# Centring all four pairs by float32r pairs, behind the attention projection's first tile

## The chip, the cores and the metric

One core of one Trainium2 chip runs the whole kernel. The metric is device time in microseconds (us), the median of several runs. The engines that matter are TensorE (PE, the matmuls; PEld is its weight load, which overlaps them), VectorE (DVE), ScalarE (ACT), GpSimd (POOL) and SyncE (SP), which here issues the loads of weights.

## What is computed

One layer of a streaming encoder with 512 tokens of 1024 features: a half-step SwiGLU, two token mixers side by side whose outputs are gated and merged, another half-step SwiGLU, and a last RMS norm. The change lies where the two mixers end. Mixer A is a delta-rule recurrence (RWKV-7) with 8 heads of 64; its output `y` is normalised per head, scaled, given a bonus, and multiplied by a gate. Mixer B is forgetting attention, also 8 heads of 64.

```python
# end of mixer A: y is (tokens, 8 heads, 64)
mu = mean(y, axis=-1); var = mean(square(y - mu), axis=-1)     # per head
y = (y - mu) * rsqrt(var + LNX_EPS)
y = y * lnx_g + lnx_b
y = (y + bonus) * (sigmoid(g_lo) @ g_up)
y_a = y @ rwkv_proj                    # 512 -> 1024
y_b = attention_output @ fox_proj      # 512 -> 1024
x = x + (sigmoid(g_A) * y_a + sigmoid(g_B) * y_b) @ w_out
```

## The kernel before, in words

Features lie on the 128 partitions and the 512 tokens along the free dimension, so a tile is 128x512 in f32, one PSUM bank. A matmul of f32 accuracy is made of float32r parts: a value is split into a high half (a cast on ACT) and a low half (a subtraction on DVE), and `mm3` (L174 to L177) adds high by high, high by low and low by high. A single matrix that is exact in float32r needs only the two parts of the other operand: `exact` (L191), two matmuls. A plain f32 matmul shows in the trace as two passes.

The stretch at issue runs from `gslot` (L1991) to `written(False)` (L2091). Two heads make a pair, so mixer A's output is four tiles `vs[0]` to `vs[3]`, slices of one buffer `V4`. For each pair p:

- `first(p)` multiplies `vs[p]` by the matrix `center` (identity less 1/64 within a head), into the bank `ycs[p]`, which comes from a PSUM pool of three (`pr`). Before, pairs 0 to 2 do this as one plain f32 matmul, and pair 3 by `exact` with a split `parts["y"]`.
- `squared(p)` squares the bank on ACT, `parts_of` or `halved` splits the square.
- `second(p)`, the norm round, sums the squares over a head (`pg`, two matmuls) and opens the gate by three float32r matmuls of the split gate codes `gl` (also named `pg` in the trace).
- `logs(p)` takes Ln and Exp on ACT, which gives 1/sqrt; `divided(p)`, `shaped(p)` and `opened(p)` are three DVE steps over `vs[p]`, and `halves_of(p)` splits the result into `ya[p]` for the RWKV projection.

Beside this runs the attention projection: `proj(m, fox_proj, ...)` for eight output tiles m, 12 matmuls each into the bank `ppj`. Its weights come by `weights()`: a load on SP into one of three raw buffers, the high half `whi` on ACT, the low half `wlo` on DVE, both with two buffers. `gated(m)` multiplies a tile by its gate on DVE and frees the bank. The loop over m lays `second`, `logs` and the steps of `ROUNDS[m]` between the tiles.

Within this stretch `dve`, `act` and `pe` are `Queued`: each instruction is put behind the one before it on its engine, so that each of the three runs in the order of the text. All of them carry line L103 in the trace, where `Queued` calls the engine; they are told apart by their tiles. The planner's list ahead of it (`plan.run(ORDER, PLACES)`, L1975) ends with the last merge gate, whose product with `rstd` (`gs`) is the last DVE instruction of that list. Instructions outside, such as the RWKV projection's weights (L167 and L168), the residual loads of POOL (L2113) and the gates' tanh (`late_tanh`, L2105), are placed by a scheduler; the first three tanh only behind `parted`, the last ACT instruction at the point m = 4 of the loop.

After the stretch comes the RWKV projection, `proj(m, rwkv_proj, ya)` for eight tiles, then the output projection and the second SwiGLU.

Of the kernel before, what the change touches and what calls it, by code (L numbers as in the profile page):

```python
# [10 lines left out]
F32R = mybir.dt.float32r  # L11
# [8 lines left out]
P = 128  # L20
T = 512
# [5 lines left out]
NP = DA // P  # L27
# [15 lines left out]
COL_Q = COL_W + 160  # L43
# [39 lines left out]
def kernel(  # L83
# [24 lines left out]
    dve, act, pe = [Queued(e, False) for e in (nc.vector, nc.scalar, nc.tensor)]  # L108
# [14 lines left out]
    def bank(name, pool_=None):  # L123
        pool_ = pool_ or pm
        return pool_.tile([P, T], F32, tag="b", name=name)

    def tmp(name, shape=(P, T), dt=F32, tag="t", **kw):
        return tp.tile(list(shape), dt, tag=tag, name=name, **kw)
# [14 lines left out]
    center = cp.tile([P, P], F32R, name="center")  # L143
# [13 lines left out]
    def load_raw(aps, kt, n):  # L157
        raw = wp.tile([P, kt, n], F32, tag="raw", name="raw", bufs=3)
        for c0, src in aps:
            loads.append(nc.sync.dma_start(raw[:, :, c0:c0 + src.shape[1]],  # L160
                                           src.rearrange("(k p) c -> p k c", p=P)))
        return raw

    def split_w(raw, kt, n, eng=None, hi_eng=None):
        hi = wp.tile([P, kt, n], F32R, tag="whi", name="whi", bufs=2)
        lo = wp.tile([P, kt, n], F32R, tag="wlo", name="wlo", bufs=2)
        (hi_eng or act).copy(hi[:], raw[:])  # L167
        (eng or dve).tensor_tensor(lo[:], raw[:], hi[:].bitcast(F32), op=ALU.subtract)  # L168
        return hi, lo
# [4 lines left out]
    def mm3(ps, whi, wlo, xhi, xlo, first, last, onto=False):  # L174
        pe.matmul(ps, whi, xhi, start=first, stop=False, skip_group_check=onto)  # L175
        pe.matmul(ps, whi, xlo, start=False, stop=False, skip_group_check=onto)  # L176
        return pe.matmul(ps, wlo, xhi, start=False, stop=last, skip_group_check=onto)  # L177
# [7 lines left out]
    def parts_of(src):  # L185
        hi, lo = tmp("shi", dt=F32R), tmp("slo", dt=F32R)
        act.copy(hi[:], src)
        dve.tensor_tensor(lo[:], src, hi[:].bitcast(F32), op=ALU.subtract)
        return hi, lo

    def exact(ps, mat, src, parts=None):  # L191
        hi, lo = parts or parts_of(src)
        pe.matmul(ps, mat[:], hi[:], start=True, stop=False)
        pe.matmul(ps, mat[:], lo[:], start=False, stop=True)

    def split(dst_hi, dst_lo, src, hi_eng="act"):
        cast = act.copy(dst_hi, src) if hi_eng == "act" else dve.tensor_copy(dst_hi, src)
        return cast, dve.tensor_tensor(dst_lo, src, dst_hi.bitcast(F32), op=ALU.subtract)

    def f32(ap):  # L200
        return ap.bitcast(F32)
# [115 lines left out]
    with tc.tile_pool(name="x0", bufs=1) as x0:  # L317
# [99 lines left out]
        for c in range(2, KD):  # L417
# [14 lines left out]
            elif c == 6:  # L432
                second = [split_w(load_raw([(0, ffn1_w1[0][:, P:2 * P])], KD, P), KD, P, qdve, hi_eng=qact)]
# [70 lines left out]
    class Seven:  # L504
# [12 lines left out]
        def second(s, g):  # L517
            d = s.lo[g][:, :, TH:]
            dve.tensor_tensor(d, d, s.hi[g][:, :, TH:], op=ALU.subtract)
# [131 lines left out]
    class Wide:  # L651
# [226 lines left out]
        def gated(s, j):  # L878
            h, t = s.seven.hidden(j), s.sa[j]
            act.activation(t, t, AF.Silu)  # L880
            dve.tensor_tensor(h, h, t, op=ALU.mult)
# [231 lines left out]
    with ExitStack() as mx:  # L1113
# [68 lines left out]
        lg = tmp("lg")  # L1182
# [33 lines left out]
        for o, c0, mu in ((spare[2], DA, 4), (spare[3], 0, 0)):  # L1216
            ps = bank("pk", pf)
# [3 lines left out]
        for p in range(NP):  # L1221
            za.append((zslots[2 * p], zslots[2 * p + 1]))
            for i, (w_, x_, par0, o) in enumerate(((uw, lw, PAR_W0, zslots[2 * p]), (ux, lx, PAR_A0, zslots[2 * p + 1]))):
                ps = bank("pz", (pr, pf)[i])
# [3 lines left out]
        logs = tc.keep_in_program_order(act.preload_act_table_set("natural_log_exp_and_others"))  # L1228
# [4 lines left out]
        t2 = pctx.enter_context(tc.tile_pool(name="t2", bufs=1, side="right"))  # L1233
# [8 lines left out]
        vs = [V4[:, p] for p in range(NP)]  # L1242
# [154 lines left out]
        t2 = fctx.enter_context(tc.tile_pool(name="fx", bufs=1, side="right"))  # L1397
# [8 lines left out]
        for t in range(C - 1):  # L1406
            n, m = t + 1, C - 1 - t
# [20 lines left out]
        class Rows(Columns):  # L1428
# [8 lines left out]
            def weights(s):  # L1437
                super().__init__("pq", s.at)
# [518 lines left out]
        ybs = []  # L1957
# [19 lines left out]
        def proj_w(m, wt):  # L1977
            return load_w([(0, wt[0][:, m * P:(m + 1) * P])], NP, P)

        def proj(m, wt, y, w=None):  # L1980
            wh, wl = w or proj_w(m, wt)
            ps = bank("ppj")
            for k in range(NP):
                mm3(ps[:], wh[:, k, :], wl[:, k, :], y[k][0], y[k][1], k == 0, k == NP - 1)
            return ps
# [9 lines left out]
        gup, lg, bons = gslot[10], gslot[11], gslot[12:16]  # L1995
# [5 lines left out]
            nc.gpsimd.dma_start(gslot[m], gsave[KD + m])  # L2001
        fws = [proj_w(0, fox_proj)]
        ycs, sqs, pgs, pus, parts = [None] * NP, [None] * NP, [None] * NP, [None] * NP, {}
        gl = [t2.tile([P, T], F32R, name=f"gl{i}", tag=tag) for i, tag in enumerate(("kb1", "klc0", "klc1", "qb1"))]

        def first(p):
            ycs[p] = bank("yc", pr)
            if p < NP - 1:
                pe.matmul(ycs[p][:], f32(center[:]), vs[p], start=True, stop=True)
            else:  # L2010
                exact(ycs[p][:], center, None, parts["y"])

        def squared(p):
            sqs[p] = gslot[8 + p % 2]
            act.activation(sqs[p], ycs[p][:], AF.Square)
# [9 lines left out]
        def logs(p):  # L2025
            rn = tslot[p]
            act.activation(rn, pgs[p][:], AF.Ln, bias=epsl[:, 0:1], scale=1.0 / 64)
            act.activation(rn, rn, AF.Exp, scale=-0.5)
# [14 lines left out]
            squared(p)  # L2043
            parts[p] = parts_of(sqs[p])

        ROUNDS = ((divided, 0), (shaped, 0), (opened, 0)), ((fourth, 3), (halves_of, 0), (divided, 1), (shaped, 1)),                  ((opened, 1), (divided, 2), (shaped, 2)), ((opened, 2), (halves_of, 1)),                  ((halves_of, 2), (divided, 3)), ((shaped, 3), (opened, 3)), ((halves_of, 3),), ()

        def gated(m, ps):
            g = gslot[m] if m + 1 < KD else gs
# [8 lines left out]
        def halved(src, tags):  # L2058
            hi, lo = [t2.tile([P, T], F32R, name="shi", tag=tag) for tag in tags]
            split(hi[:], lo[:], src)  # L2060
            return hi, lo

        parts["y"] = halved(vs[3], [f"qk{COL_Q}{i}" for i in range(2)])
        weights()
        for p in range(3):
            first(p)
        for p in range(2):
            squared(p)
            parts[p] = parts_of(sqs[p])
        for i, src in enumerate((gup, lg)):  # L2070
            split(gl[2 * i][0:96, :], gl[2 * i + 1][0:96, :], src[0:96, :])
        squared(2)
        parts[2] = halved(sqs[2], [f"qk{COL_Q}{i}" for i in range(2, 4)])
        ps = proj(0, fox_proj, ybs, fws[0])
        for m in range(KD):
            if m < NP:
                second(m)
            gated(m, ps)
            if m + 2 < KD:
                weights()  # L2080
            if m < NP:
                logs(m)
            if m == NP:
                parted = act.last
            for do, p in ROUNDS[m]:
                do(p)
            if m + 1 < KD:
                ps = proj(m + 1, fox_proj, ybs, fws[m + 1])
            if m == 0:
                first(3)  # L2090
        written(False)  # L2091
        fctx.close()
# [25 lines left out]
        for m in range(KD):  # L2118
            g = slot[m]
            ps = proj(m, rwkv_proj, ya)  # L2120
# [4 lines left out]
        for m in range(KD):  # L2125
            wh, wl = load_w([(0, w_out[0][:, m * P:(m + 1) * P])], KD, P)
            ps = bank("pw")
# [69 lines left out]
    with tc.tile_pool(name="hp", bufs=1) as hp:  # L2197
# [5 lines left out]
        ps = [bank("pa"), bank("pb", pr)]  # L2203
# [51 lines left out]
```

## Time and profile before

| | us |
|---|---|
| median of 3 runs | 1066.22 |
| lowest and highest | 1064.59, 1066.35 |
| the profiled execution | 1066.64 |
| its span in the trace | 1064.9 |
| PE busy in the span | 1054.1 |
| DVE, ACT, POOL busy | 842.8, 712.0, 243.4 |

The profile is of one execution. Its span lies 1.7 us below that execution's own time, which includes what lies around the span, and the execution lies 0.42 us above the median. Starts are given from the span's start. A matmul's listed duration includes its way through the array: matmuls that follow each other without a gap start 0.227 us apart but last 0.39, so a bank is complete 0.39 us after its last matmul's start. The chain's times are those of ends, some tenths later than the timeline's starts.

### The profile page before, as it was taken

The numbers are of one execution on the slowest core, as the hardware profiler recorded it, in microseconds if no ns is written. First come the engines' busy times: TensorE is split into PE (matmuls) and PEld (weight loads), VectorE is DVE, ScalarE is ACT, GpSimd is POOL, SyncE is SP. The second block draws the span as 40 slices with busy tenths as digits, with TensorE's granted clock in tenths as the row PEclk, the third lists the DMA queues.
The fourth block names the chain that finished last, engine by engine and source line by source line (L and its number), as shares of the span: only waits on it lengthen the run. The fifth ranks groups of instructions, "written<-read, shape, count | busy, mean of one in ns | idle before, by whom it ended". The sixth has DMA issues, their size and how long they took to land.

```text
span 1064.9 us, 16739 instructions
## 1 busy us (share of the span) xinstructions
PE 1054.1 (99%) x6178; PEld 863.2 (81%) x6178; DVE 842.8 (79%) x1171; ACT 712.0 (67%) x1107; POOL 243.4 (23%) x291
## 2 busy tenths in 40 slices
PE   9999999999999999999999999999999999999997
PEld 7888888888887887878777877888888888888886
DVE  7997776789865698878989878866797766799874
ACT  6767868776555766435888766554578868676554
POOL 1221220134203201312012231136321212115210
PEclk9999999999999999999999999999999999999999
DMA  7989989889945433443335565566989999979972
GB/s 213 264 181 237 231 201 255 198 194 193 232 123 170 116 112 97 129 121 117 86 74 125 130 177 164 189 167 163 283 200 204 208 239 232 201 212 206 236 186 79
DMA packets 194960, 190.25 MB, mean 179 GB/s; under 512 B 64958, under 2 KB 131070, under 8 KB 194878
## 3 DMA queue, kind: packets, MB, share of 16 engines
q1 hardware_dynamic: 147230, 110.78, 36.3%
q0 software_dynamic: 33392, 70.14, 34.2%
q10 hardware_dynamic: 14256, 8.26, 2.7%
q8 instruction: 49, 0.80, 0.3%
q14 instruction: 33, 0.27, 0.1%
HBM read 163.51 MB, written 12.52 MB: 165 GB/s over the span
## 4 chain that ended last, share of the span: by engine, by line
PE 92%; DVE 4%; DMA 1%; ACT 1%; issue 1%; SPq 0%; DVEq 0%; ACTq 0%; POOL 0%; POOLq 0%
PE P L103 39%; PE P L177 6%; PE P L176 6%; PE P L175 6%; PE pgt L103 5%; PE spot L103 3%; PE pq L103 3%; PE l L103 2%; PE ppj L103 2%; PE pb L103 2%; PE pa L103 2%; PE pk L175 1%; PE pk L176 1%; PE pw L176 1%; PE pk L177 1%; PE pw L177 1%
## 5 line engine op out<-in xcount | busy, mean ns | idle before, releaser
L103 PE MATMUL P<-sraw,q 128*128 128x512 f32 x344 | 91.3, 389 | 0.0
L103 PEld LDWEIGHTS P<-sraw,q 128*128 128x128 f32 x344 | 64.6, 188 | 13.4
L103 PE MATMUL P<-swhi,q 128*128 128x512 f32 x224 | 71.2, 389 | 0.0
L167 ACT CAST whi<-raw 128x1024 fp32r<-128x1024 f32 (+2 forms) x42 | 40.3, 960 | 44.1 <-issue 14.2
L103 PE MATMUL P<-sraw,wxh 128*128 128x512 f32 x200 | 67.7, 390 | 0.0
L694 POOL DMA_DIRECT2D cb<-in_ffn_w_dram x20 | 24.1, 1207 | 142.3 <-DVE cd L103 74.9
L103 PE MATMUL P<-swhi,wxh 128*128 128x512 f32 x144 | 56.6, 393 | 0.0
L168 DVE TENSOR_TENSOR wlo<-raw,whi 128x1024 fp32r<-128x1024 f32 (+2 forms) x43 | 48.4, 1126 | 10.1 <-ACT whi L167 8.9
L103 PE MATMUL P<-swhi,wxl 128*128 128x512 f32 x144 | 56.1, 390 | 0.0
L103 PE MATMUL P<-swlo,wxh 128*128 128x512 f32 x144 | 56.1, 389 | 0.0
L694 POOL DMA_DIRECT2D cd<-in_ffn_w_dram x24 | 29.3, 1221 | 115.3 <-DVE swlo L103 37.9
L103 PE MATMUL P<-sraw,wxl 128*128 128x512 f32 x136 | 52.9, 389 | 0.0
L103 PEld LDWEIGHTS P<-swhi,q 128*128 128x128 f32 x224 | 42.0, 188 | 8.8 <-DVE q L103 0.2
L103 ACT COPY RD<-spot 32x128 f32<-32x128 f32 (+2 forms) x128 | 39.8, 311 | 11.3 <-PE spot L103 9.3
L103 DVE TENSOR_TENSOR u<-P,u 128x512 f32<-128x512 f32 x52 | 33.4, 682 | 17.2 <-ACT u L103 17.2
L103 PEld LDWEIGHTS P<-sraw,wxh 128*128 128x128 f32 x200 | 37.5, 188 | 7.8
L103 PE MATMUL P<-swlo,q 128*128 128x512 f32 x112 | 43.6, 389 | 0.0
L552 POOL DMA_DIRECT2D ca<-in_ffn_w_dram x16 | 19.3, 1205 | 96.1 <-DVE swlo L103 66.7
L177 PE MATMUL pk<-xh,wlo 128*128 128x512 f32 x96 | 37.5, 392 | 1.0 <-DVE wlo L168 1.0
L175 PE MATMUL pk<-xh,whi 128*128 128x512 f32 x96 | 38.1, 397 | 0.4 <-DVE u L1261 0.4
L176 PE MATMUL pk<-xl,whi 128*128 128x512 f32 x96 | 37.5, 390 | 0.0
L177 PE MATMUL P<-swhi,wxl 128*128 128x512 f32 x96 | 37.3, 389 | 0.0
(632 smaller groups left out, 3445.6 us busy)
## 6 DMA issues: line engine op xcount, KB each, us to landing
cc<-in_ffn_w_dram SPq DMA_DIRECT2D x36, 512.0 KB
cb<-in_ffn_w_dram POOLq DMA_DIRECT2D x36, 512.0 KB, 6.6
cb<-in_ffn_w_dram SPq DMA_DIRECT2D x32, 512.0 KB
cd<-in_ffn_w_dram POOLq DMA_DIRECT2D x32, 512.0 KB, 7.5
ca<-in_ffn_w_dram POOLq DMA_DIRECT2D x32, 512.0 KB, 8.7
raw<-in_w_in_dram SPq DMA_DIRECT2D x27, 512.0 KB
ca<-in_ffn_w_dram SPq DMA_DIRECT2D x20, 512.0 KB
cd<-in_ffn_w_dram SPq DMA_DIRECT2D x18, 512.0 KB
```

Of the source, the lines that this page charges most:

```text
L103: q.last = do(*a, **kw)
L167: (hi_eng or act).copy(hi[:], raw[:])
L168: (eng or dve).tensor_tensor(lo[:], raw[:], hi[:].bitcast(F32), op=ALU.subtract)
L175: pe.matmul(ps, whi, xhi, start=first, stop=False, skip_group_check=onto)
L176: pe.matmul(ps, whi, xlo, start=False, stop=False, skip_group_check=onto)
L177: return pe.matmul(ps, wlo, xhi, start=False, stop=last, skip_group_check=onto)
L552: nc.gpsimd.dma_start(s.sum[g], src, accum_op=ALU.add)
L694: nc.gpsimd.dma_start(to, s.block(b, n, h), accum_op=ALU.add)
```

## The change

All four pairs are centred by `exact`, with the split of their outputs made ahead by `centred(p, tags)`. The first attention tile goes ahead of the centrings of pairs 0 to 2. The squares and splits that follow, and the split gate codes, move to m = 0 behind `gated(0)`; pair 3's output is split at m = 0 too and centred behind tile 2 instead of tile 1. `second` and `logs` are called one tile later, for m from 1 to 4 instead of 0 to 3, and `ROUNDS` is moved by one tile, with the last steps drawn together: `shaped(3)` joins `divided(3)` at m = 5, and `opened(3)` and `halves_of(3)` stand together at m = 6. The tiles `gl` are taken only after the centrings, since two of their buffers hold the split of pair 2 before.

```diff
-        gl = [t2.tile([P, T], F32R, name=f"gl{i}", tag=tag) for i, tag in enumerate(("kb1", "klc0", "klc1", "qb1"))]
+        gl = []
         def first(p):
             ycs[p] = bank("yc", pr)
-            if p < NP - 1:
-                pe.matmul(ycs[p][:], f32(center[:]), vs[p], start=True, stop=True)
-            else:
-                exact(ycs[p][:], center, None, parts["y"])
+            exact(ycs[p][:], center, None, parts["y", p])
...
-        ROUNDS = ((divided, 0), (shaped, 0), (opened, 0)), ((fourth, 3), (halves_of, 0), (divided, 1), (shaped, 1)),                  ((opened, 1), (divided, 2), (shaped, 2)), ((opened, 2), (halves_of, 1)),                  ((halves_of, 2), (divided, 3)), ((shaped, 3), (opened, 3)), ((halves_of, 3),), ()
+        ROUNDS = (), ((divided, 0), (shaped, 0), (opened, 0)), ((fourth, 3), (halves_of, 0), (divided, 1), (shaped, 1)), \
+            ((opened, 1), (divided, 2), (shaped, 2)), ((opened, 2), (halves_of, 1)), \
+            ((halves_of, 2), (divided, 3), (shaped, 3)), ((opened, 3), (halves_of, 3)), ()
...
-        parts["y"] = halved(vs[3], [f"qk{COL_Q}{i}" for i in range(2)])
+        def centred(p, tags):
+            parts["y", p] = halved(vs[p], tags)
+
+        quarters = [f"qk{COL_Q}{i}" for i in range(4)]
+        for p, tags in enumerate((quarters[0:2], quarters[2:4], ("kb1", "klc0"))):
+            centred(p, tags)
         weights()
+        ps = proj(0, fox_proj, ybs, fws[0])
         for p in range(3):
             first(p)
-        for p in range(2):
-            squared(p)
-            parts[p] = parts_of(sqs[p])
-        for i, src in enumerate((gup, lg)):
-            split(gl[2 * i][0:96, :], gl[2 * i + 1][0:96, :], src[0:96, :])
-        squared(2)
-        parts[2] = halved(sqs[2], [f"qk{COL_Q}{i}" for i in range(2, 4)])
-        ps = proj(0, fox_proj, ybs, fws[0])
         for m in range(KD):
-            if m < NP:
-                second(m)
+            if 0 < m <= NP:
+                second(m - 1)
             gated(m, ps)
+            if m == 0:
+                for p in range(2):
+                    squared(p)
+                    parts[p] = parts_of(sqs[p])
+                gl.extend(t2.tile([P, T], F32R, name=f"gl{i}", tag=tag) for i, tag in enumerate(("kb1", "klc0", "klc1", "qb1")))
+                for i, src in enumerate((gup, lg)):
+                    split(gl[2 * i][0:96, :], gl[2 * i + 1][0:96, :], src[0:96, :])
             if m + 2 < KD:
                 weights()
-            if m < NP:
-                logs(m)
+            if m == 0:
+                squared(2)
+                parts[2] = halved(sqs[2], quarters[2:4])
+                centred(3, quarters[0:2])
+            if 0 < m <= NP:
+                logs(m - 1)
             if m == NP:
                 parted = act.last
             for do, p in ROUNDS[m]:
                 do(p)
             if m + 1 < KD:
                 ps = proj(m + 1, fox_proj, ybs, fws[m + 1])
-            if m == 0:
+            if m == 1:
                 first(3)
```

## Rows read from the trace of the kernel before

**Rows 1.** The page, part 1: busy time, share of the span, instructions of each engine.
```profile
PE 1054.1 (99%) x6178; PEld 863.2 (81%) x6178; DVE 842.8 (79%) x1171; ACT 712.0 (67%) x1107; POOL 243.4 (23%) x291
```
**Rows 2.** The chain that ended last, 620 to 700 us: start, us, what.
```profile
643.11 2.58 PE yc L103 x6
645.69 2.77 PE ppj L103 x12
...
649.61 2.75 PE ppj L103 x12
...
660.60 1.15 PE pg L103 x5
661.75 10.91 PE ppj L103 x48
```
**Rows 3.** Timeline of PE, 636 to 676 us: start, us, engine, line, out<-in.
```profile
642.95 2.74 PE L103 MATMUL yc<-V,center 128*128 128x512 f32 x6
...
648.30 0.39 PE L103 MATMUL pg<-shi,bonesr 128*128 128x512 f32 x1
...
652.19 0.62 PE L103 MATMUL yc<-shi,center 128*128 128x512 f32 x2
...
664.33 0.39 PE L103 MATMUL ppj<-yh,whi 128*128 128x512 f32 x1
...
672.49 0.39 PE L175 MATMUL ppj<-ya,whi 128*128 128x512 f32 x1
```
**Rows 4.** Timeline of DVE, the same stretch; in brackets idle before and releaser.
```profile
643.15 0.69 DVE L103 TENSOR_TENSOR gs<-pgt,rstd 128x512 f32<-128x512 f32 x1 [1.50 <-PE pgt L103]
643.76 0.68 DVE L103 TENSOR_TENSOR wlo<-raw,whi 128x512 fp32r<-128x512 f32 x1
...
647.05 1.28 DVE L103 TENSOR_TENSOR gl<-G,gl 96x512 fp32r<-96x512 f32 x2
...
650.44 0.68 DVE L103 TENSOR_TENSOR V<-yc,Tall 128x512 f32<-128x512 f32 x1
```
**Rows 5.** Timeline of ACT, the same stretch.
```profile
640.22 0.62 ACT L103 CAST whi<-raw 128x512 fp32r<-128x512 f32 x1
...
642.92 0.62 ACT L103 CAST whi<-raw 128x512 fp32r<-128x512 f32 x1 [1.56 <-PE pgt L103]
644.01 0.60 ACT L103 ACTIVATE G<-yc 128x512 f32<-128x512 f32 x1 [0.47 <-PE yc L103]
...
649.02 0.68 ACT L103 ACTIVATE Tall<-pg,epsl 128x512 f32<-128x512 f32 x1
649.73 0.63 ACT L103 ACTIVATE Tall<-Tall 128x512 f32<-128x512 f32 x1
```
**Rows 6.** Timeline of DVE at an earlier PE wait, 417 to 426 us.
```profile
423.89 1.22 DVE L168 TENSOR_TENSOR wlo<-raw,whi 128x1024 fp32r<-128x1024 f32 x1
```
**Rows 7.** Timeline of PE at the same wait.
```profile
425.16 0.50 PE L177 MATMUL pk<-xh,wlo 128*128 128x512 f32 x1 [0.68 <-DVE wlo L168]
425.50 0.40 PE L175 MATMUL pk<-xh,whi 128*128 128x512 f32 x1
```
**Rows 8.** DMA issues, 630 to 680 us: count, KB each, median us to landing.
```profile
G<-gsave POOLq DMA_DIRECT2D x5, 256.0 KB, 5.4
```
**Rows 9.** Timeline of ACT toward the end of the stretch.
```profile
664.30 0.62 ACT L103 CAST whi<-raw 128x512 fp32r<-128x512 f32 x1 [1.34 <-PE ppj L103]
664.83 0.61 ACT L103 CAST ya<-V 128x512 fp32r<-128x512 f32 x1
665.46 1.28 ACT L2105 ACT_TABLE_LOAD   x1
666.76 1.68 ACT L2105 ACTIVATE ga<-ga 128x512 f32<-128x512 f32 x3
668.34 0.60 ACT L103 CAST whi<-raw 128x512 fp32r<-128x512 f32 x1
```
**Rows 10.** Timeline of DVE toward the end of the stretch.
```profile
671.57 0.68 DVE L168 TENSOR_TENSOR wlo<-raw,whi 128x512 fp32r<-128x512 f32 x1
672.17 0.68 DVE L103 TENSOR_TENSOR ya<-V,ya 128x512 fp32r<-128x512 f32 x1
```

## The prediction

> **What bounds the kernel now.** I read the page first, then the chain of work that ended last, then the timelines of TensorE (PE), VectorE (DVE) and ScalarE (ACT) around the edit. PE is busy for 99% of the span [rows 1], so a microsecond of PE streaming that goes, or a PE wait that comes, moves the end by about as much. The chain shows the same at the edit: PE alone from the centring matmuls to the first RWKV projection tile, with no other engine between [rows 2]. In this stretch everything on DVE, ACT and PE is chained in the order in which the code writes it. DVE shows that the chain is strict: it idles 1.50 us until the last gate column is out of PE (`gs`), and only then splits the first projection weight (`wlo`), whose high half ACT had written three microseconds before [rows 4, 5].
>
> **The passes.** Before, three plain f32 centrings run as six passes of 2.58 us together [rows 2]. The float32r pairs need six passes too, at the pace of the other float32r matmuls, 10.91/48 = 0.227 us, so 1.36 us. The gain is 1.22 us, on PE, so on the path. Pair 3 has its float32r pair already and keeps it. Nothing else on PE changes in size.
>
> **The first tile ahead of the centrings.** It would start at 642.95, where the centrings start now [rows 3]. Its first two matmuls read the high weight, ready since 640.8 [rows 5]. The third reads the low weight, and is due at 643.40. DVE finishes that at 643.76 + 0.68 = 644.44, behind `gs` [rows 4]; `gs` waits for the gate's last matmul, which the edit doesn't touch. Today the 2.58 us of centrings cover this wait; that cover is gone. What a PE wait for such a weight costs is shown elsewhere in the trace: a low weight written at 423.89 + 1.22 = 425.11, its matmul at 425.16, the next at 425.50, 0.39 us after the write [rows 6, 7]. So the fourth matmul starts at 644.83 instead of 643.63: **+1.20 us**. The ends: nothing, if DVE splits the weight in its idle 1.50 us (a rival below), and 1.5 us, that idle row, if the pick-up is worse. I take 1.20. Gain and wait cancel: the tile and the centrings end at 648.30 - 1.22 + 1.20 = 648.28, where the tile alone ends now [rows 3]. The three casts and low halves of the pairs' outputs that come ahead cost nothing: ACT idles 1.56 us up to 642.92 in the trace [rows 5], and DVE writes the low halves at 644.4 to 646.3 behind `wlo`, before PE needs the first at 646.9.
>
> **The squares, one step later.** Pair 0's square needs its centring, whose second pass starts at 646.9 + 0.23 and ends 0.39 later, so it starts at 647.6 instead of 644.01 [rows 5]. ACT's list behind it is the old one with two casts more (the fourth weight, pair 3's output), 0.53 us each in a run of casts [rows 9]. DVE's low halves of the gate codes (`gl`) move as much: 647.05 + 3.57 = 650.62, both done at 651.9 [rows 4]. PE reaches the first norm round (`pg`) after tile 1 of 2.75 us [rows 2], at 651.03, and its fourth matmul, due at 651.71, reads the last of these halves. It waits to 651.95: **+0.24 us** (0 to 0.5, by what ACT's list may slip).
>
> **Pair 3's centring and its bank.** `first(3)` takes the PSUM bank of pair 0 out of a pool of three, so it waits for `divided(0)`. Now this is done a microsecond before it is needed (650.44 + 0.68 against 652.19 [rows 3, 4]). After the change ACT's Ln for pair 0 comes at 649.02 + 3.57 + 1.06 = 653.65, its Exp 0.71 later, done at 655.0, and `divided(0)` at 655.07 to 655.75 [rows 4, 5]. PE, with 1.15 us for a norm round [rows 2], is through tile 2 at 651.03 + 1.15 + 0.24 + 2.75 = 655.17 and waits to 655.80: **+0.63 us** (0.3 to 1.0). Everything behind it on PE, norm round 1 and tile 3, is delayed by this.
>
> Up to here the sum is -1.22 + 1.20 + 0.24 + 0.63 = **+0.85 us**. The weights' loads on SyncE keep their order; each is released by the low half three tiles earlier, 7.5 us or more ahead of its cast, and a transfer of 256 KB lands in 5.4 us [rows 8], so none becomes late. GpSimd's residual loads wait for pair 3's low half and move with it; the whole RWKV projection, 22 us, lies ahead of their first use.
>
> **The tail.** Round 3 now stands one tile nearer to the RWKV projection. In the trace the table load and three tanh go between a cast and the last attention weight (`whi` at 668.34) [rows 9], and they may start only behind ACT's last instruction at m = 4, which the edit makes Exp of pair 3. Tile 5 starts at 664.33 + 0.85 = 665.18 [rows 3], round 3 1.15 ahead of it, at 664.03; its Ln comes 0.23 + 0.39 us later and a hand-over behind, at 664.7, Exp at 665.4, pair 1's cast at 666.0, table and tanh at 666.6 to 669.6 (1.28 + 1.68 us), the weight's cast at 669.5, its low half at 670.1 to 670.8. PE needs that at 671.1, so it just holds. But behind it DVE's order now has pair 2's low half, `divided(3)`, `shaped(3)`, the gate of tile 6 and `opened(3)`, at 0.60 us a start and 0.71 where one reads the last (before, only three of the five came behind it). The first RWKV weight's low half (L168, not in the chain) stands right ahead of pair 3's low half in the trace [rows 10], so it would follow `opened(3)`: 673.9 to 674.6. PE begins the RWKV projection at 672.49 + 0.85 = 673.34 [rows 3] and needs it at 673.79; its fourth matmul starts at 674.58 + 0.39 = 674.97 instead of 674.02. **+0.95 us**, between 0 (the weight's cast ahead of a tanh) and 2.35 (a rival).
>
> In the trace the first tanh starts 0.02 us after the table load's end, and the load 0.02 after the cast before it [rows 9]. The Trainium skill, "ScalarE: Activation LUTs", What ACT_TABLE_LOAD costs, gives each switch a drain of about 1380 ns beside the load's 1283 ns. By that the tail's wait would be 0.95 + 1.38 = 2.33 us and the change +3.2 us, as an estimate from that page; the load's length agrees with the row, the drain has no place in it.
>
> **The sum.** -1.22 + 1.20 + 0.24 + 0.63 + 0.95 = +1.8 us. The profiled execution took 1066.64 us with a span of 1064.9; it would take 1068.4. It lies 0.42 us above the median of the runs, 1066.22, so I forecast **1068.0**.
>
> **Rivals.**
> *No wait in the tail* (1067.1, chance 0.27): the last attention weight's cast goes ahead of one or two tanh, whose place the scheduler chooses; each is worth 0.53 us. For it: the cast's buffer is free from 668.1 (tile 5's end), before the second tanh. Against it: in the trace all three went ahead, though the buffer was free at 667.2.
> *A longer tail* (1069.4, chance 0.13, slower than before): the first RWKV weight's low half is put behind pair 3's low half. That needs `opened(3)`, a cast of 0.62 and itself, so it ends at 675.4, the weight's at 676.0, and PE loses 2.35 us instead of 0.95: +3.2 us. It decides from the moment at which DVE finds pair 3's cast done when `opened(3)` ends. Against it: in the trace the weight goes ahead [rows 10].
> *The first tile doesn't wait* (1065.9 to 1066.8, chance 0.10): DVE splits the first weight ahead of `gs`. Then all comes 1.2 us earlier: -1.22 + 0.24 + 0.63 = -0.35, with the tail's 0.95 or without. Against it: the chain's order, unedited, kept DVE idle 1.50 us.
> *ACT stands still behind the table load* (1069.3, chance 0.02): if it does so for as long as the load itself, 1.28 us [rows 9], the last attention weight and all behind it on DVE come that much later, PE loses 0.95 + 1.28 = 2.23 us there, and the change costs 3.1 us. The two rows 0.02 us apart speak against it. This is the drain of the Trainium skill's page named above.
> *The pure gain* (1065.0, chance 0.04): the passes go and no wait appears; this needs both the order of DVE and ACT's list to be otherwise.
>
> **How the numbers follow.** The forecast has 0.44. Below it lie 1067.1, 1066.4 and 1065.0, above it 1069.4. A difference of about 0.2%, 2.1 us, is what a measurement of this kernel can tell from no change. No case gains that much; 0.02 is left for what I don't see. Slower by that: the longer tail (0.13), the still table (0.02) and the part of the forecast in which the bounds of the waits and the runs' own spread (1064.59 to 1066.35) add half a microsecond, a fifth of 0.44: 0.24. The rest, 0.74, is no difference. From 1065.7 to 1069.5 are nearly all of the forecast and of the case without the tail's wait, over half of the two outer ones: 0.8.
>
> **What would show it.** Centring passes at 0.23 us in one row of six behind the first tile; a PE wait of over a microsecond on `wlo` at the first tile's third matmul; short PE waits at the first norm round and at pair 3's centring, the latter named after DVE `V`; and a PE wait on L168's `wlo` in the first RWKV tile. If the first of these waits is missing, the forecast is wrong by 1.2 us; if the last is, by 0.95.

## The result, and the profile after

| us | before | after |
|---|---|---|
| median (lowest to highest), 13 runs each | 1065.83 (1064.59 to 1069.11) | 1067.59 (1066.25 to 1068.66) |
| ratio, 95% interval | | 1.0017, 1.001 to 1.0024 |
| the profiled execution, its span | 1066.64, 1064.9 | 1067.78, 1066.1 |
| the stretch of the edit | 51.30 | 53.08 |

The change costs 1.76 us by the medians. The forecast was 1.8 us, at 1068.0 from a median of 1066.22; the 13 runs put that median at 1065.83.

A single profiled execution differs from the next by a microsecond or two, so the spans alone are too coarse here. I therefore measure one stretch in each trace. It begins where the first matmul after the last gate column is due (0.227 us behind the start of that column's last matmul, tile `pgt`) and ends with the start of the output projection's first matmul (tile `pw`). All that the edit moves lies in it. It grew by 53.08 - 51.30 = 1.78 us, which agrees with the medians. Behind it both executions take the same time to the end of the span, 370.7 and 370.6 us. The spans differ by 1.2 us only because this execution of the changed kernel reached the stretch 0.57 us earlier.

The page of the changed kernel, part 1, beside [rows 1]:

```profile
PE 1053.5 (99%) x6178; PEld 862.2 (81%) x6178; DVE 845.1 (79%) x1174; ACT 713.9 (67%) x1110; POOL 244.7 (23%) x291
```

PE is busy for 0.6 us less, in a span 1.2 us longer: streaming went, waiting came. DVE and ACT have three instructions more each, the low and high halves of three pairs' outputs.

The chain that ended last, changed kernel, 636 to 680 us (start, us, what), beside [rows 2]:

```profile
643.19 0.69 DVE wlo L103
643.93 2.60 PE ppj L103 x10
...
647.03 0.61 ACT G L103
...
653.38 0.68 DVE G L103
654.06 0.60 DVE wlo L103
654.66 0.61 DVE V L103
655.32 0.73 PE yc L103 x2
```

Before, this stretch was PE from end to end. Now the chain leaves PE twice. It passes over DVE's split of the first weight, and then over ACT and DVE from the first centring's square to the step `divided(0)` (`V`), which frees the bank of pair 3's centring.

The timeline of PE, changed kernel (start, us, engine, line, out<-in, count; in brackets the idle time and its releaser), beside [rows 3]:

```profile
642.61 0.39 PE L103 MATMUL ppj<-yl,whi 128*128 128x512 f32 x1
643.93 0.50 PE L103 MATMUL ppj<-yh,wlo 128*128 128x512 f32 x1 [0.93 <-DVE wlo L103]
644.27 0.40 PE L103 MATMUL ppj<-yh,whi 128*128 128x512 f32 x1
...
646.37 1.57 PE L103 MATMUL yc<-shi,center 128*128 128x512 f32 x6
647.77 0.40 PE L103 MATMUL ppj<-yh,whi 128*128 128x512 f32 x1
...
650.96 1.18 PE L103 MATMUL pg<-gl,gl 96*128 96x512 f32 x3
651.98 0.40 PE L103 MATMUL ppj<-yh,whi 128*128 128x512 f32 x1
...
654.49 0.39 PE L103 MATMUL ppj<-yh,wlo 128*128 128x512 f32 x1
655.32 0.73 PE L103 MATMUL yc<-shi,center 128*128 128x512 f32 x2 [0.44 <-DVE V L103]
655.89 0.40 PE L103 MATMUL pg<-shi,bonesr 128*128 128x512 f32 x1
...
672.81 0.39 PE L103 MATMUL ppj<-yh,wlo 128*128 128x512 f32 x1
673.18 0.47 PE L175 MATMUL ppj<-ya,whi 128*128 128x512 f32 x1
...
676.61 0.39 PE L176 MATMUL ppj<-ya,whi 128*128 128x512 f32 x1
```

Read it by the distance between starts, since a matmul's listed length hides short waits. Without a wait it is 0.227 us. What goes beyond that, with the 0.1 us by which the next matmul still lags after a wait:

- the six passes: 647.77 - 646.37 = 1.40 us instead of 2.58, so **-1.18**
- the first tile's third matmul: 643.93 - 642.61 - 0.23 = 1.09, and 0.11 at the next, **+1.20**
- norm round 0: 651.98 - 650.96 = 1.02 for three matmuls of 0.68, **+0.34**
- pair 3's centring: 0.60 and 0.12 behind it, **+0.72**
- the beginning of the RWKV projection: 676.61 - 672.81 = 3.80 for fourteen matmuls of 0.227, **+0.6** in four small waits with what lags behind them

The sum is +1.7. The trace's list of PE waits names only the first and the third of them, 0.93 and 0.44 us, because it counts from the modelled end of the matmul before. The others show in the distances, and in the timeline of the weight loads (PEld), which gives the idle time before each load and its releaser:

```profile
651.41 0.30 PEld L103 LDWEIGHTS pg<-gl,gl 96*128 96x128 f32 x2 [0.48 <-DVE gl L103]
...
673.15 0.19 PEld L175 LDWEIGHTS ppj<-ya,whi 128*128 128x128 f32 x1 [0.38 <-issue]
...
673.69 0.19 PEld L177 LDWEIGHTS ppj<-ya,wlo 128*128 128x128 f32 x1 [0.24 <-DVE wlo L168]
...
675.67 0.19 PEld L176 LDWEIGHTS ppj<-ya,whi 128*128 128x128 f32 x1 [0.30 <-DVE ya L103]
...
676.27 0.19 PEld L175 LDWEIGHTS ppj<-ya,whi 128*128 128x128 f32 x1 [0.30 <-DVE G L103]
```

The idle time of a load isn't PE's loss: the load at 673.69 stood for 0.24 us, and its matmul started in time, only the next one 0.08 late. "issue" stands where the profile shows no releaser.

The timeline of DVE in the changed kernel, beside [rows 4, 10]:

```profile
643.19 0.68 DVE L103 TENSOR_TENSOR wlo<-raw,whi 128x512 fp32r<-128x512 f32 x1
...
650.07 1.28 DVE L103 TENSOR_TENSOR gl<-G,gl 96x512 fp32r<-96x512 f32 x2
...
654.58 0.68 DVE L103 TENSOR_TENSOR V<-yc,Tall 128x512 f32<-128x512 f32 x1
...
672.35 0.68 DVE L103 SCALAR_TENSOR_TENSOR G<-G,ppj 128x512 f32<-128x512 f32 x1
672.95 0.68 DVE L168 TENSOR_TENSOR wlo<-raw,whi 128x512 fp32r<-128x512 f32 x1
673.55 0.68 DVE L103 TENSOR_TENSOR V<-V,pg 128x512 f32<-128x512 f32 x1
```

And that of ACT toward the end of the stretch, beside [rows 9]:

```profile
665.62 0.60 ACT L103 CAST ya<-V 128x512 fp32r<-128x512 f32 x1
666.24 1.28 ACT L2113 ACT_TABLE_LOAD   x1
667.54 1.67 ACT L2113 ACTIVATE ga<-ga 128x512 f32<-128x512 f32 x3
669.12 0.60 ACT L103 CAST whi<-raw 128x512 fp32r<-128x512 f32 x1
```

Each of the first three PE waits ends a twentieth of a microsecond behind a DVE write. The weight's low half is done at 643.19 + 0.68 = 643.87, PE goes on at 643.93; `divided(0)` is done at 655.26, PE goes on at 655.32. The gate codes are done at 650.07 + 1.28 = 651.35; PE's row groups the three matmuls, but the weight load of the one that waited starts at 651.41. In the tail the order on ACT is as in [rows 9] (cast, table load, three tanh, then the last attention weight's cast), only now DVE's list behind that weight ends so late that PE meets it.

### The profile page after: what moved, and what is told of

It reads as the page before. It is cut to its first block, busy times and chain, and to the rows that moved or that the text cites. A ratio compares the mean times of both kernels' runs of the same rounds, so it can differ in the third digit from the quotient of the medians.

```text
span 1066.1 us, 16746 instructions
## 1 busy us (share of the span) xinstructions
PE 1053.5 (99%) x6178; PEld 862.2 (81%) x6178; DVE 845.1 (79%) x1174; ACT 713.9 (67%) x1110; POOL 244.7 (23%) x291
## 4 chain that ended last, share of the span: by engine, by line
PE 92%; DVE 4%; ACT 1%; DMA 1%; issue 1%; SPq 0%; DVEq 0%; ACTq 0%; POOL 0%; POOLq 0%
PE P L103 39%; PE P L177 6%; PE P L175 6%; PE P L176 6%; PE pgt L103 5%; PE spot L103 3%; PE pq L103 3%; PE l L103 2%; PE pk L175 2%; PE pk L177 2%; PE pb L103 2%; PE pk L176 2%; PE pa L103 2%; PE ppj L103 2%; PE pw L176 1%; PE pw L177 1%
## 5 line engine op out<-in xcount | busy, mean ns | idle before, releaser
L168 DVE TENSOR_TENSOR wlo<-raw,whi 128x1024 fp32r<-128x1024 f32 (+2 forms) x43 | 48.5, 1128 | 10.3 <-ACT whi L167 9.1
```

## The experiments

Each ran 11 times beside the kernel before, whose median was 1065.98 beside runs 1 to 4 and 1066.05 beside runs 5 to 7. A ratio is to the kernel before. The stretch is that of the one profiled execution. The code is shortened; `...` marks what is left out.

**1. The first weight split ahead of the last gate step.** Theory: the 1.2 us wait in the first tile is DVE's order and nothing else. In the changed kernel, tile 0's weight is split just ahead of the last DVE instruction of the planner's list (`gs`):

```diff
...
-        plan.run(ORDER, PLACES)
+        gate = [plan.ops[n] for n in ORDER if plan.ops[n]["engine"] == "DVE"][-1]
+        plan.run(ORDER, PLACES, lambda o: fws.append(load_w(...)) if o is gate else None)
...
-        fws = [proj_w(0, fox_proj)]
...
```

> The kernel after, with one thing moved: the first projection weight is split ahead of the last gate column's product (gs) on DVE, in DVE's idle time, so that PE's first tile finds it. The stretch from the end of the last gate column to the output projection's first matmul took 51.30 us before and 53.08 after. The theory (PE pays four waits that DVE's and ACT's order puts before it, the first of them 1.20 us on this weight): this wait goes, the three others stay as they are, since all that follows moves forward together; stretch 51.9, whole kernel 1.2 us below the kernel after, so 0.5 to 0.6 above before. Rival (the wait is only a place: what PE would meet next is late as well, the low halves of the pairs' outputs behind gs, or ACT's list): the later waits grow by what the first gives back; stretch 53.0, nothing gained.

Measured: 1066.38 us, ratio 1.0003 (0.9994 to 1.0012), stretch 51.78. The timeline of DVE in this kernel:

```profile
642.07 0.69 DVE L103 TENSOR_TENSOR wlo<-raw,whi 128x512 fp32r<-128x512 f32 x1
643.65 0.69 DVE L103 TENSOR_TENSOR gs<-pgt,rstd 128x512 f32<-128x512 f32 x1 [0.89 <-PE pgt L103]
```

The split takes place in DVE's idle time, which falls from 1.50 to 0.89 us, and is done at 642.76, before the tile begins at 643.45. The stretch falls by 1.30, the wait's 1.20 and 0.1 beside it. The other waits stay at 0.36, 0.71 and some 0.6.

**2. The same move in the kernel before.** It tells whether the move is a gain of its own.

> The kernel before with the same move. The theory (in before the centrings cover this wait wholly): stretch 51.3, no difference in time (within 0.1 us). Rival (the early split is a gain by itself, whatever stands in front of PE): the stretch falls by up to 1.2 us.

Measured: 1065.92 us, 1.0001 (0.9992 to 1.0009), stretch 51.29 against 51.30. Before the change the wait for this weight lay under the 2.58 us of centrings and cost nothing. The move is worth 1.3 us only where the edit has taken that cover away.

**3. The gate codes early.** In the changed kernel, the tiles `gl` are taken at the start and split before the centrings. Pair 2's output, which held two of their buffers, is split elsewhere:

```diff
...
-        for p, tags in enumerate((quarters[0:2], quarters[2:4], ("kb1", "klc0"))):
+        for p, tags in enumerate((quarters[0:2], quarters[2:4])):
             centred(p, tags)
+        parts["y", 2] = parts_of(vs[2])
         weights()
+        for i, src in enumerate((gup, lg)):
+            split(gl[2 * i][0:96, :], gl[2 * i + 1][0:96, :], src[0:96, :])
...
```

> The kernel after, with the split of the gate codes taken out of the squares' list and put ahead of the centrings, where ACT idles 4.1 us (pair 2's output takes other buffers for that). ACT's list before the first Ln is 1.05 us shorter. The theory (the second wait, 0.34 us, is on the gate codes' low half, the third, 0.72 us, on pair 0's bank, which divided(0) frees at the end of ACT's list): both go, stretch 53.08 - 1.06 = 52.0; the first wait stays at 1.2 and the tail at 0.6. Rival (the third wait is set by DVE's own queue ahead of divided(0), the gate of tile 1 and a weight, not by ACT's list): only the second goes, stretch 52.7.

Measured: 1066.29 us, 1.0006 (0.9997 to 1.0014), stretch 52.02, which is 1.06 less than the change as it is. The waits at norm round 0 and at pair 3's centring are both gone; the first tile's 1.20 and the tail stay. So these two have one cause: ACT's and DVE's list behind the first centring, in which the four instructions on the gate codes stood.

**4. The tanh one tile later.** In the changed kernel, the table load and the first three tanh may start only behind ACT's last instruction at m = 5:

```diff
-            if m == NP:
+            if m == NP + 1:
                 parted = act.last
```

> The kernel after, with the first three tanh (and their table load) allowed only one tile later, so that the last attention weight's cast goes ahead of them; nothing else moves, and DVE's order is the same. The theory (the tail's four short waits, 0.6 us together in the first RWKV tile, come from that cast being 1.3 us late behind table and tanh, which pushes DVE's list of five into the RWKV projection): the tail's waits go or shrink to 0.1, stretch 52.5; the three waits in front stay. Rival (the tail is late because round 3 stands one tile nearer to the projection, whatever ACT does between): the waits stay, stretch 53.1.

Measured: 1067.03 us, 1.0012 (1.0 to 1.0023), stretch 52.39, which is 0.69 less. The timeline of ACT in this kernel:

```profile
667.37 0.62 ACT L103 CAST whi<-raw 128x512 fp32r<-128x512 f32 x1 [1.34 <-PE ppj L103]
...
668.53 1.28 ACT L2113 ACT_TABLE_LOAD   x1
669.83 1.68 ACT L2113 ACTIVATE ga<-ga 128x512 f32<-128x512 f32 x3
```

The last attention weight is cast ahead of the table load, and all four waits at the beginning of the RWKV projection are gone. So the tail's loss comes from the load and the tanh that stand ahead of that cast. In the kernel before they stood there too, at no cost [rows 9]; it takes the later list of the changed kernel as well.

**5. All three together.**

> The kernel after with all three cures: the first projection weight split ahead of gs, the gate codes split where ACT idles, the tanh one tile later. The theory (four waits of their own, which add up, on a change that saves 1.2 us of passes): the cures give 1.30 + 1.06 + 0.69 as they did alone, stretch 53.08 - 3.05 = 50.0, and the kernel is 1.2 us faster than before, near 0.999 of it. Rival (the waits share slack, so that curing all gives less than the sum): stretch between 50.5 and 51.5, no faster than before.

Measured: 1064.24 us beside 1066.05, ratio 0.9984 (0.9975 to 0.9993), stretch 50.10. The chain in this kernel:

```profile
642.70 2.72 PE ppj L103 x12
645.42 1.40 PE yc L103 x6
646.82 2.73 PE ppj L103 x12
```

PE alone again, with no wait in the attention projection, the centrings or the RWKV projection. Taken one by one the three were worth 1.30 + 1.06 + 0.69 = 3.05 us; together they are worth 53.08 - 50.10 = 2.98. So the waits stand one behind the other and add up. What is left against the kernel before is -1.20 us, the six passes. This kernel is faster than the one before, by an interval that excludes no change. The changed kernel didn't run beside it, but its own interval lies on the other side.

**6. The passes alone, in the old order.** The kernel before with float32r pairs for all four centrings, still ahead of the first tile:

```diff
-            if p < NP - 1:
-                pe.matmul(ycs[p][:], f32(center[:]), vs[p], start=True, stop=True)
-            else:
-                exact(ycs[p][:], center, None, parts["y"])
+            exact(ycs[p][:], center, None, parts["y", p])
...
+        for p in range(2):
+            parts["y", p] = halved(vs[p], [f"qk{COL_Q}{i}" for i in range(2 * p, 2 * p + 2)])
+        parts["y", 2] = parts_of(vs[2])
         weights()
...
```

> The kernel before with float32r pairs for all four pairs, and the old order: centrings first, rounds where they were, first tile behind. The theory (what the pairs save on PE is paid by waiting for their low halves, which DVE can write only behind gs): PE waits 1.9 us for pair 0's low half and little for the others, the centrings end 1.1 us later than before; ACT's squares come 2.1 us later, and the gate codes' low half 0.4 us too late for the first norm round; stretch 52.8 (52.4 to 53.0), 1.5 us above before. Rival (the pairs are the gain, and only the edit's new order cost time): stretch 50.1, 1.2 us below before.

Measured: 1067.58 us, 1.0016 (1.0007 to 1.0024), stretch 53.83. The direction is the theory's; the size is the theory's 1.5 us by the medians, but 2.53 us in the profiled execution. The timeline of PE in this kernel:

```profile
642.85 0.40 PE L103 MATMUL yc<-shi,center 128*128 128x512 f32 x1
645.00 1.63 PE L103 MATMUL yc<-shi,center 128*128 128x512 f32 x4 [1.75 <-DVE shi L103]
646.42 0.63 PE L103 MATMUL yc<-slo,center 128*128 128x512 f32 x1
646.85 0.63 PE L103 MATMUL ppj<-yh,whi 128*128 128x512 f32 x1
```

The table of windows of the same kernel (stretch, length, busy us of PE, PEld, DVE, ACT and POOL, granted clock, DMA share, GB/s):

```profile
643.00:645.00 2.00, 0.25 (x3) 0.00 (x1) 1.95 (x4) 0.44 (x1) 0.54 (x1) 1.00 1.05 402
645.00:647.00 2.00, 2.00 (x6) 1.30 (x7) 2.00 (x4) 1.94 (x4) 0.00 (x0) 0.71 1.02 373
647.00:649.00 2.00, 2.00 (x7) 1.54 (x6) 1.98 (x4) 1.97 (x5) 0.00 (x0) 0.50 0.76 220
```

PE waits 645.00 - 642.85 - 0.23 = 1.92 us for pair 0's low half, which stands behind `gs` and the weight on DVE. That is the cover that the edit gets by putting the first tile ahead. Then something comes that no theory had: the granted clock falls to 0.50 (1.2 GHz), and matmuls start 0.43 us apart. From 645.00 to 649.35 there are eleven of them, 4.35 us instead of 2.50: 1.85 us more. The sum -1.18 + 1.92 + 1.85 = +2.59 answers the measured 53.83 - 51.30 = +2.53. But not all of the 1.85 is the clock's. The weight loads wait twice more in it, for the low halves of pairs 1 and 2:

```profile
645.60 0.30 PEld L103 LDWEIGHTS yc<-shi,center 128*128 128x128 f32 x2 [0.30 <-DVE shi L103]
...
646.20 0.29 PEld L103 LDWEIGHTS yc<-slo,center 128*128 128x128 f32 x1 [0.31 <-DVE slo L103]
```

At full clock, with 0.34 for the matmul that waited last and 0.227 for the six behind it, PE would be at 646.20 + 0.34 + 1.36 = 647.90 where it is at 649.35. By this estimate 1.45 us are the clock's and 0.40 those two waits', and at full clock the stretch would be 53.83 - 1.45 = 52.4, the lower end of what was expected. The wait for the gate codes that was expected isn't in the rows: DVE has done their last half at 648.59 + 1.28 = 649.87, and PE begins with them at 651.19. This profiled execution took 1069.08 us, 1.5 us above the median of the runs. That is about the clock's price, but run 1's profiled execution lies 1.15 us above its median with no fall of the clock there. Whether the clock falls in every execution isn't known.

**7. The splits ahead, in the old order.** As 6, but the outputs of pairs 0 to 2 are split ahead of `gs` on DVE and ahead of the first weight's cast on ACT, in other buffers (the function `ahead` is called from the planner's list, as in 1):

```diff
...
+        def ahead():
+            for p, tags in enumerate(([f"qk{COL_Q}{i}" for i in range(2, 4)], ["tr", "tr"])):
+                hi, lo = [t2.tile([P, T], F32R, name="yv", tag=tag, ...) for tag in tags]
+                split(hi[:], lo[:], vs[p])
+                parts["y", p] = hi, lo
+            parts["y", 2] = parts_of(vs[2])
...
```

> As the passes alone, but the splits of pairs 0 to 2 stand ahead of gs on DVE and ahead of the first weight's cast on ACT, in other buffers; pair 3's split and everything behind stay where they were in before. The theory (all that is needed is that DVE writes the low halves in its idle 1.5 us; the edit's new order is not): PE finds the low halves, the first weight comes just in time, the gate codes' low half perhaps 0.15 us late; stretch 50.1 to 50.3, 1.0 to 1.2 us below before. Rival (the idle 1.5 us is too short for three low halves and gs, so that gs and the first weight move back and PE waits there): stretch 50.8 to 51.3, no gain.

Measured: 1065.33 us, 0.9995 (0.9986 to 1.0004), stretch 50.73. The timeline of DVE in this kernel:

```profile
641.52 0.69 DVE L103 TENSOR_TENSOR slo<-V,shi 128x512 fp32r<-128x512 f32 x1
642.13 0.69 DVE L103 TENSOR_TENSOR gs<-pgt,rstd 128x512 f32<-128x512 f32 x1
...
645.73 1.28 DVE L103 TENSOR_TENSOR gl<-G,gl 96x512 fp32r<-96x512 f32 x2
```

And that of PE, at norm round 0:

```profile
646.32 0.39 PE L103 MATMUL pg<-gl,gl 96*128 96x512 f32 x1
647.07 0.73 PE L103 MATMUL pg<-gl,gl 96*128 96x512 f32 x2 [0.36 <-DVE gl L103]
647.63 0.40 PE L103 MATMUL ppj<-yh,whi 128*128 128x512 f32 x1
```

The three low halves fill DVE's idle 1.50 us and a little more (`gs` starts 0.43 us into the stretch instead of 0.20), and the centrings run without a wait, so the passes gain their 1.2 us here as well. But DVE's list has no gap left from there to the gate codes, whose last half is done at 647.01. PE waits for it, 0.52 + 0.11 = 0.63 us. What is left is 50.73 - 51.30 = -0.57: half of the gain, too little for the medians to tell from none. That lies between the two expected ranges: DVE's idle time is too short, as the rival said, but PE waits for the gate codes and not for the first weight.

## Why the prediction was right

The sign, the size and most of the places were right; the tail was right in its cause and wrong in its form.

- **The passes**: -1.18 measured, -1.22 forecast. Runs 5 and 7 show that the gain is real wherever no wait takes it back.
- **The first tile ahead of the centrings**: +1.20 measured and forecast. The price came from a PE wait elsewhere in the trace [rows 6, 7], and run 1 shows the cause by taking it away. The rival *the first tile doesn't wait* needed just that order, and the change doesn't make it.
- **The squares, one step later**: +0.34 for +0.24, and **pair 3's centring and its bank**: +0.72 for +0.63. Both a tenth higher, within the bounds given, for one reason: the working has the matmul behind a wait start 0.34 instead of 0.23 us later in its first term, and left this 0.11 out of these two. The waits alone were 0.23 and 0.60. Run 3 shows that they are one list's lateness. For the second, DVE's own list had a part too: the chain ends with the gate of tile 1, a weight and `divided(0)` one behind the other on DVE, where the working counted ACT's steps alone. The forecast's sum to this point was +0.85; measured, -1.18 + 1.20 + 0.34 + 0.72 = +1.08.
- **The tail**: +0.6 for +0.95, and here a step failed. I put the first RWKV weight's low half (L168) behind `opened(3)`, since it had stood right ahead of pair 3's low half [rows 10]. It went one place further ahead: 672.95, with `opened(3)` at 673.55. So the wait on it is there, as the load at 673.69 names it, but it cost 0.08 us instead of 0.95. The rest of the tail is three other waits on the same late list. The loads at 675.67 and 676.27 name pair 3's low half (`ya`) and the gate of tile 7 (`G`), which frees the second tile's bank. The one at 673.15 has no releaser; by its time and the two banks of the tiles' pool (`pm`) it waits for the gate of tile 6, done at 672.35 + 0.68 = 673.03, which is argued and not shown. That the table load and the tanh hold up the last attention weight and DVE's list behind it is shown by run 4, in which all four go.
- **The sum**: +1.8 forecast, +1.78 in the stretch. The tail was 0.35 too high, the other terms 0.23 too low and 0.1 is not put down to any wait, so part of the agreement is luck.
- **ACT stands still behind the table load**: it didn't. The load ends at 666.24 + 1.28 = 667.52 and the first tanh starts at 667.54; in run 4 they stand 0.02 us apart too. The drain that the Trainium skill, "ScalarE: Activation LUTs", What ACT_TABLE_LOAD costs, adds to a switch isn't in these rows.
- *The pure gain* is what run 5 reaches, with the orders of DVE and of ACT's list both changed, as that rival said it would need.

## What to carry to other kernels

When PE bounds a kernel, the price of a slow matmul is only what no other wait would fill. Before making it faster, list what comes due under it (here a weight's low half, and the squares behind it) and move those first. After a reordering read the distances between matmul starts and the idle times of the weight loads, not only the named waits of PE. The waits here stood one behind the other on PE and added up, so each could be removed and priced by a run of its own.

## What the runs showed of the hardware

A PE wait can cost more than its length. In run 6 PE had been streaming at a granted clock of 1.00, then waited 1.92 us, with 0.25 us busy of the 2.00 up to 645.00. Behind the wait the granted clock fell: 0.71 over the next 2 us and 0.50, the 1.2 GHz level, over the 2 us after them. The slower matmuls added some 1.45 us, the estimate of run 6, to the wait's 1.92. In the changed kernel the first tile lost 1.20 us to a wait, and the clock stayed at 1.00, as the table of windows shows:

```profile
643.00:645.00 2.00, 1.07 (x5) 0.88 (x6) 2.00 (x5) 0.00 (x0) 0.00 (x0) 1.00 1.03 366
```

What of the two cases decides it is open; no run varied the wait alone.
